# The low parts of 56 weight blocks in the state space part: on VectorE in place of GpSimd

## The chip, the cores and the metric

One core of one Trainium2 chip. The metric is device time in microseconds (us) of one launch, and where several launches were made, their median. Engines are named as in the profile: PE is TensorE's matmul stream and PEld its weight loads, DVE is VectorE, ACT is ScalarE, POOL is GpSimd, SP is SyncE, which issues most DMAs. [...]

## What is computed

One layer of a hybrid diffusion backbone: 512 latent tokens and 256 context tokens of 1024 channels, one combined input projection, a bidirectional gated linear attention branch (GLA, 4 heads) and a bidirectional Mamba-2 branch (SSD, 4 groups of 8 heads), a gated merge, an output projection and a SwiGLU feed-forward part. The change lies in the SSD branch. Cut to it, the reference is:

```python
def _ssd_scan(x, bm, cm, a, s0):
    def step(S, inp):
        xi, bi, ci, ai = inp
        cum = jnp.cumsum(ai, axis=1)
        seg = cum[:, :, None] - cum[:, None, :]
        Lm = jnp.exp(jnp.where(mask, seg, -jnp.inf))
        cb = jnp.einsum('btgn,bsgn->btsg', ci, bi)
        y = jnp.einsum('btsg,btsge,bsgep->btgep', cb, Lm, xi)
        y = y + jnp.einsum('btgn,bgenp->btgep', ci, S) * jnp.exp(cum)[..., None]
        S_new = jnp.exp(cum[:, -1])[..., None, None] * S + jnp.einsum(
            'bsgn,bsge,bsgep->bgenp', bi, jnp.exp(cum[:, -1:] - cum), xi)
        return S_new, y
...
def _mixer(parts, lp, init, conv_fn):
    ...
    o_b, st_bf, st_bb = _bidir(_ssd_scan, (x_f, sb, sc, a_f), (x_b, sb, sc, a_b), init[2], init[3])
    o_b = o_b + lp['d_skip'].reshape(SSM_GROUPS, SSM_HPG, 1) * xh
    o_b = o_b.reshape(Bn, L, SSM_INNER) * jax.nn.silu(z)
    o_b = rms_norm(o_b.reshape(Bn, L, SSM_GROUPS, SSM_INNER // SSM_GROUPS), ...)
    y_b = o_b @ lp['w_pb']
    merged = jax.nn.sigmoid(gate_a) * y_a + jax.nn.sigmoid(gate_b) * y_b
    return merged @ lp['w_out'], (st_af, st_ab, st_bf, st_bb)
```

## The kernel before, in words

All weights come in blocks of 128 partitions x 1024 fp32 numbers. A matmul with fp32 weights is made as three float32r products: the weight is split into a high part `whi` (ACT, a copy that rounds, line 188) and a low part `wlo = raw - whi` (line 189, in `split_w`), the activations likewise, and PE sums hi x hi, hi x lo and lo x hi. `load_raw` (line 176) lets SP fetch the raw block into one of 3 buffers; `whi` and `wlo` have 2 buffers each. A Python list, `split_pool`, says which engine makes the low part: DVE, or POOL while its element is true.

The stages are, with rough times in the profiled execution: loading and the adaptive modulation, GLA heads 0 to 3 (to 400 us), then the SSD branch group by group. `ssd_proj(g)` makes group g's projections: `bm` (1 block), `cm` (1), `xs` (4 blocks) and the gate `z` (4 blocks). Its PE tiles are `l_bm`, `l_xs` (latent tokens), `c_xs` (context tokens) and `r_z` (tokens as rows, four token chunks, two banks). The `xs`, `bm` and `cm` columns go through a convolution on ACT and DVE (`cv_...`, line 663) and are transposed (`tr_x`). `ssd_chain(g)` does the scan in 4 chunks of 128 tokens. Per chunk it makes four tiles `E` (DMA from `cdr`, DVE line 747; a masked copy, line 749), two products `yi` that DVE scales (line 773) and adds to `y` (774), adds the `y` products (775), multiplies by `z` (776), and normalises: ACT sums squares, DVE makes `rv_y` (168), POOL the power `rr_y` (170), DVE scales `y` by it (783). PE then transposes `y` to `yT` (line 501 is a helper through which all these small PE products go), ACT copies it to the high part (788) and DVE makes the low part (789). `proj_back` (lines 632 to 638) multiplies a group's `yT` by the blocks `pb` and DVE adds the result to `acc_b`. It is written behind the projections of the next group, so that it lies beside that group's chain.

After group 3 come the last blocks of the two merge gates (`ga`, `gb`; line 918 on), a transpose `adaT` of the modulation (929), which goes to DRAM and comes back as `sh` and `sc` rows (942), a row of norm weights `n` (DMA on SP, 950) by which DVE multiplies `sc` (952), and `proj_back` of group 3 with the merge of each column block (`tgm`, 969 to 978). Then come the output projection and the feed-forward part, to the end.

[...] PE has 4 banks for the large products (`mm`) and 4 for the small ones (`sm`).

Of the kernel before, what the change touches and what calls it, by code (L numbers as in the profile page):

```python
# [129 lines left out]
def hybrid_layer_kernel(ctx: ExitStack, tc: tile.TileContext, x, xc, wts, vec, rows, up, msk, lvl, out):  # L130
# [48 lines left out]
    split_pool = [False]  # L179
# [497 lines left out]
    def ssd_proj(g):  # L677
        bc = pj.tile([P, 2, SEQ], F32, tag="p4", name=f"bc_{g}")
        lat, cx = proj_cols(("bm", g), True)
        bT = conv_silu(6 * g + 4, lat, cx, f"b_{g}")  # L680
        nc.gpsimd.tensor_copy(bc[:, 0, :], bT[:, 0:SEQ])
        bt = pj.tile([P, 6, P], F32, tag="p3", name=f"bt_{g}")
        to_rows(bT, bt, f"b_{g}")
        lat, _ = proj_cols(("cm", g), False)
        conv_silu(6 * g + 5, lat, None, f"c_{g}", dst=bc[:, 1, :])
        xt = pj.tile([P, 6, 512], F32, tag="x12", name=f"x_{g}")
        for j in range(4):
            lat, cx = proj_cols(("xs", g, j), True)
            xT = conv_silu(6 * g + j, lat, cx, f"x_{g}_{j}")
            to_rows(xT, xt[:, :, j * P:(j + 1) * P], f"x_{g}_{j}")  # L690
        z = [ch.tile([P, 512], F32, tag="z", name=f"z_{g}_{i}", bufs=4) for i in range(4)]
        for c in range(2):
            banks = proj_rows(lambda kh: ("z", g, c, kh), 4)
            for i in range(4):
                pv = banks[i // 2][:, (i % 2) * 256:(i % 2) * 256 + 256]
                zv = z[i][:, c * 256:(c + 1) * 256]
                nc.scalar.activation(zv, pv, AF.Tanh, scale=0.5)
                nc.vector.scalar_tensor_tensor(zv, zv, 1.0, pv, ALU.add, ALU.mult)  # L698
        return bc, bt, xt, z
# [189 lines left out]
    pr, _ = gla_proj(3)  # L889
    early_gate()  # L890
    gla_chain(3, *pr, oH1, oL1)
    split_pool[0] = True
    sp = ssd_proj(0)
    proj_back(lambda c: ("pa", 1, c), oH1, oL1, acc_a, False)
    nc.gpsimd.dma_start(ydr, acc_a)
# [13 lines left out]
    yy = back_pair("yT_3")  # L909
    ssd_chain(3, *sp, *yy)  # L910

    split_pool[0] = False

    for j in range(n_early[0], 8):
        ya = pj.tile([P, SEQ], F32, tag="cva", name=f"ya_{j}")
# [286 lines left out]
```

## Time and profile before

| | |
|---|---|
| median of 3 launches | 1431.89 us (1430.45 to 1432.89) |
| profiled execution, its own time | 1434.66 us |
| its span, first to last instruction | 1432.9 us |
| mean granted clock | 0.981 |
| PE busy | 1357.3 us (95%) |
| DVE busy | 871.0 us (61%) |
| ACT busy | 502.2 us (35%) |
| POOL busy | 465.4 us (32%) |

The profile comes from one execution, taken by the hardware profiler. Its own time is 1.8 us more than its span, which is what lies around the first and the last instruction, and 2.8 us more than the median of the launches without a profiler. Matmuls overlap in the pipeline, so a matmul's printed duration is longer than the distance to the next; the distances between their starts tell the pace. In the name of a group, "x" and a number is a count of instructions, and behind "<-" stands what ended a wait.

### The profile page before, as it was taken

The numbers are of one execution on the slowest core, as the hardware profiler recorded it, in microseconds if no ns is written. First come the engines' busy times: TensorE is split into PE (matmuls) and PEld (weight loads), VectorE is DVE, ScalarE is ACT, GpSimd is POOL, SyncE is SP. The second block draws the span as 40 slices with busy tenths as digits, with TensorE's granted clock in tenths as the row PEclk, the third lists the DMA queues.
The fourth block names the chain that finished last, engine by engine and source line by source line (L and its number), as shares of the span: only waits on it lengthen the run. The fifth ranks groups of instructions, "written<-read, shape, count | busy, mean of one in ns | idle before, by whom it ended". The sixth has DMA issues, their size and how long they took to land.

```text
span 1432.9 us, 19032 instructions
## 1 busy us (share of the span) xinstructions
PE 1357.3 (95%) x7462; PEld 1152.4 (80%) x7462; DVE 871.0 (61%) x1292; ACT 502.2 (35%) x828; POOL 465.4 (32%) x333
## 2 busy tenths in 40 slices
PE   5999999999999999999899899999789999999997
PEld 3798999899888778877877787877578888888886
DVE  4559676563785787569758866766883343433225
ACT  6464333433444223433322342322243222222222
POOL 1355554245234433543253334113651122100001
PEclk9899999999999999999899999999999999999999
DMA  9363323334231343232322332557423333333331
GB/s 367 124 211 108 95 92 112 102 104 144 70 96 60 125 126 96 74 109 83 96 70 84 98 110 78 173 168 253 147 87 101 120 118 116 120 117 91 101 103 73
DMA packets 58010, 169.19 MB, mean 118 GB/s; under 512 B 6064, under 2 KB 10304, under 8 KB 57792
## 3 DMA queue, kind: packets, MB, share of 16 engines
q1 hardware_dynamic: 55328, 157.96, 34.0%
q0 software_dynamic: 2304, 9.64, 2.1%
q8 instruction: 59, 0.97, 0.3%
q10 hardware_dynamic: 288, 0.36, 0.1%
q14 instruction: 31, 0.25, 0.1%
HBM read 156.23 MB, written 11.72 MB: 117 GB/s over the span
## 4 chain that ended last, share of the span: by engine, by line
PE 66%; DVE 15%; DMA 9%; issue 6%; ACT 2%; POOL 2%; SPq 1%; POOLq 0%; DVEq 0%; ACTq 0%
DMA E<-cdr 5%; PE up L1056 3%; PE gate L1055 3%; PE gate L1056 3%; PE up L1055 3%; PE gate L1054 3%; PE up L1054 3%; PE db L204 3%; PE db L206 3%; PE db L205 3%; DVE E L747 2%; PE lv L501 2%; PE r_z L386 1%; PE pb_pb L632 1%; PE pb_pb L634 1%
## 5 line engine op out<-in xcount | busy, mean ns | idle before, releaser
L341 POOL TENSOR_TENSOR raw_ada<-raw_ada,cs 128x1024 f32<-128x1024 f32 x32 | 63.7, 1990 | 279.5 <-DMA raw_ada<-in_wts_dram 227.9
L747 DVE TENSOR_TENSOR E<-E,ebias 128x512 f32<-128x512 f32 x64 | 54.7, 859 | 49.4 <-DMA E<-cdr 49.3
L386 PE MATMUL r_z<-whi_z,hH 128*128 128x256 f32 x256 | 75.7, 298 | 6.6 <-DVE z L698 6.6
L343 POOL TENSOR_TENSOR raw_ada<-raw_ada 128x512 f32<-128x512 f32 x64 | 80.0, 1250 | 4.3
L388 PE MATMUL r_z<-whi_z,hL 128*128 128x256 f32 x256 | 76.9, 301 | 0.0
L387 PE MATMUL r_z<-wlo_z,hH 128*128 128x256 f32 x256 | 74.7, 293 | 0.0
L1054 PE MATMUL gate<-h2H,whi_gate 128*128 128x512 f32 (+1 forms) x192 | 71.8, 374 | 0.0
L1055 PE MATMUL gate<-h2L,whi_gate 128*128 128x512 f32 (+1 forms) x192 | 71.7, 373 | 0.0
L1056 PE MATMUL gate<-h2H,wlo_gate 128*128 128x512 f32 (+1 forms) x192 | 71.5, 373 | 0.0
L189 POOL TENSOR_TENSOR wlo_xs<-raw_xs,whi_xs 128x1024 fp32r<-128x1024 f32 x16 | 43.1, 2693 | 63.8 <-ACT whi_xs L188 63.8
L1056 PE MATMUL up<-h2H,wlo_up 128*128 128x512 f32 x160 | 63.0, 394 | 0.0
L1055 PE MATMUL up<-h2L,whi_up 128*128 128x512 f32 x160 | 62.3, 389 | 0.0
L1054 PE MATMUL up<-h2H,whi_up 128*128 128x512 f32 x160 | 62.2, 389 | 0.0
L189 DVE TENSOR_TENSOR wlo_gate<-raw_gate,whi_gate 128x1024 fp32r<-128x1024 f32 x20 | 33.2, 1661 | 45.2 <-ACT whi_gate L188 45.2
L189 DVE TENSOR_TENSOR wlo_down<-raw_down,whi_down 128x1024 fp32r<-128x1024 f32 x18 | 22.0, 1225 | 62.4 <-ACT whi_down L188 62.3
L386 PEld LDWEIGHTS r_z<-whi_z,hH 128*128 128x128 f32 x256 | 50.9, 200 | 9.2 <-DVE z L698 7.3
L170 POOL TENSOR_TENSOR rr_f<-rv_f,negh 128x1 f32<-128x1 f32 x4 | 2.6, 662 | 168.5 <-DVE rv_f L168 168.5
L189 POOL TENSOR_TENSOR wlo_z<-raw_z,whi_z 128x1024 fp32r<-128x1024 f32 x16 | 39.4, 2462 | 53.5 <-ACT whi_z L188 51.4
L386 PE MATMUL r_v<-whi_v,hH 128*128 128x256 f32 x192 | 55.7, 290 | 1.0 <-ACT whi_v L188 1.0
L205 PE MATMUL db<-wlo_down,fH 128*128 128x512 f32 x142 | 55.2, 389 | 0.0
L206 PE MATMUL db<-whi_down,fL 128*128 128x512 f32 x142 | 55.2, 389 | 0.0
L388 PE MATMUL r_v<-whi_v,hL 128*128 128x256 f32 x192 | 55.1, 287 | 0.0
(475 smaller groups left out, 4460.1 us busy)
## 6 DMA issues: line engine op xcount, KB each, us to landing
raw_ada<-in_wts_dram SPq DMA_DIRECT2D x32, 512.0 KB, 3.6
E<-cdr SPq DMA_DIRECT2D x64, 256.0 KB, 3.4
raw_gate<-in_wts_dram SPq DMA_DIRECT2D x22, 512.0 KB, 3.6
raw_up<-in_wts_dram SPq DMA_DIRECT2D x22, 512.0 KB, 3.5
raw_down<-in_wts_dram SPq DMA_DIRECT2D x22, 512.0 KB, 3.5
aw<-in_wts_dram SPq DMA_DIRECT2D x8, 1024.0 KB, 15.4
raw_xs<-in_wts_dram SPq DMA_DIRECT2D x16, 512.0 KB, 3.6
raw_z<-in_wts_dram SPq DMA_DIRECT2D x16, 512.0 KB, 3.7
```

What stands on the lines that cost most here:

```text
L189: (nc.gpsimd if split_pool[0] else nc.vector).tensor_tensor(lo, raw, hi.bitcast(F32), ALU.subtract)
L205: nc.tensor.matmul(out_, aH, bL, start=False, stop=False)
L206: nc.tensor.matmul(out_, aL, bH, start=False, stop=stop)
L341: nc.gpsimd.tensor_tensor(raw, raw, cs[:, :, 0:1].to_broadcast([P, KD, P]), ALU.mult)
L343: nc.gpsimd.tensor_tensor(raw[:, 0:n, :], raw[:, 0:n, :], raw[:, n:2 * n, :], ALU.add)
L386: nc.tensor.matmul(o, hH[:, kk, tk], hi[:, k, :], start=st, stop=False, skip_group_check=True)
L387: nc.tensor.matmul(o, hH[:, kk, tk], lo[:, k, :], start=False, stop=False, skip_group_check=True)
L388: nc.tensor.matmul(o, hL[:, kk, tk], hi[:, k, :], start=False, stop=sp, skip_group_check=True)
L747: nc.vector.tensor_tensor(ed, ed, ebias[:, d, n, hh].unsqueeze(2).to_broadcast([P, EH, P]), ALU.add)
L1054: nc.tensor.matmul(pts[kj][:, tk], hi[:, k, :], h2H[:, k, tk], start=(k == 0), stop=False)
L1055: nc.tensor.matmul(pts[kj][:, tk], hi[:, k, :], h2L[:, k, tk], start=False, stop=False)
L1056: nc.tensor.matmul(pts[kj][:, tk], lo[:, k, :], h2H[:, k, tk], start=False, stop=(k == KD - 1))
```

## The change

Two lines are taken out, so `split_pool` stays false from the first group's projections to the end of the last group's chain:

```diff
@@ -889,7 +889,6 @@
     pr, _ = gla_proj(3)
     early_gate()
     gla_chain(3, *pr, oH1, oL1)
-    split_pool[0] = True
     sp = ssd_proj(0)
     proj_back(lambda c: ("pa", 1, c), oH1, oL1, acc_a, False)
     nc.gpsimd.dma_start(ydr, acc_a)
@@ -909,7 +908,6 @@
     yy = back_pair("yT_3")
     ssd_chain(3, *sp, *yy)
 
-    split_pool[0] = False
 
     for j in range(n_early[0], 8):
         ya = pj.tile([P, SEQ], F32, tag="cva", name=f"ya_{j}")
```

With that, line 189 runs on DVE for 56 blocks: 40 of the four groups' `bm`, `cm`, `xs` and `z`, 4 of `pa`, 12 of `pb` of groups 0 to 2. The gates `ga` and `gb`, `pb` of group 3 and the output projection had their low parts on DVE already; 4 blocks of the feed-forward part keep theirs on POOL. In the order of the instructions, DVE's rows of line 189 go from 119 to 175 and POOL's from 60 to 4. Up to the first group's projections (about 350 us) and in the feed-forward part each engine keeps its order; between these, the scheduler orders all engines anew. Behind the first line taken out, line numbers are 1 less, behind the second 2 less. Three places show what moved.

DVE, between the end of group 2's chain (`y_2`: its chunk with z tile `z_3_6306`) and group 3's projections (`z_3_7431`, fed by `r_z`). Before:

```order
L774 TENSOR_TENSOR y_2_6967<-y_2_6967,yi_2_6976 128x512
L775 TENSOR_TENSOR y_2_6967<-y_2_6967,y_3_6958 128x512
L747 TENSOR_TENSOR E_0_1_1_7858<-E_0_1_1_7858,ebias 128x512
L776 TENSOR_TENSOR y_2_6967<-y_2_6967,z_3_6306 128x512
L749 COPY_PREDICATED E_0_1_1_7858<-le_78,E_0_1_0_7855 128x512
L747 TENSOR_TENSOR E_1_0_0_7917<-E_1_0_0_7917,ebias 128x512
L168 TENSOR_SCALAR rv_y_6983<-yss_3_6981 128x1
L783 SCALAR_TENSOR_TENSOR y_2_6967<-y_2_6967,rr_y_6985,snw_6680 128x512
```

and of the change:

```order
L774 TENSOR_TENSOR y_2_6967<-y_2_6967,yi_2_6976 128x512
L749 COPY_PREDICATED E_0_1_1_7858<-le_78,E_0_1_0_7855 128x512
L775 TENSOR_TENSOR y_2_6967<-y_2_6967,y_3_6958 128x512
L747 TENSOR_TENSOR E_1_0_0_7917<-E_1_0_0_7917,ebias 128x512
L776 TENSOR_TENSOR y_2_6967<-y_2_6967,z_3_6306 128x512
L189 TENSOR_TENSOR wlo_pb_0_7669<-raw_pb_0_7670,whi_pb_0_7668 128x1024
L747 TENSOR_TENSOR E_1_0_1_7920<-E_1_0_1_7920,ebias 128x512
L168 TENSOR_SCALAR rv_y_6983<-yss_3_6981 128x1
L698 SCALAR_TENSOR_TENSOR z_3_7431<-z_3_7431,r_z_0_0_1_7433 128x256
L749 COPY_PREDICATED E_1_0_1_7920<-le_78,E_1_0_0_7917 128x512
L783 SCALAR_TENSOR_TENSOR y_2_6967<-y_2_6967,rr_y_6985,snw_6680 128x512
```

Between the last sum with `yi` and the scaling of line 783 stand nine rows in place of six, and one of the added ones is a low part. On PE, between the second `yi` product of this chunk and its `yT`, 48 `r_z` matmuls stand where 69 stood.

PE, at the end of the last `gb` block (`l_gb`), where group 3's `pb` (`pb_pb`) begins. Before; here `yT_3_8113`, the transpose of the scan's last chunk, stands 28 matmuls further up, and 52 matmuls lie between the last `yi` and it:

```order
L366 MATMUL l_gb_8507<-hH,wlo_gb_8502 128x512
L929 MATMUL adaT<-idt,ada 96x128
L632 MATMUL pb_pb_0_0_8580<-yT_7804,whi_pb_0_8574 128x512
L633 MATMUL pb_pb_0_0_8580<-yT_7804,whi_pb_0_8574 128x512
L632 MATMUL pb_pb_0_1_8605<-yT_7804,whi_pb_0_8574 128x512
L633 MATMUL pb_pb_0_1_8605<-yT_7804,whi_pb_0_8574 128x512
```

and of the change:

```order
L366 MATMUL l_gb_8507<-hH,wlo_gb_8502 128x512
L501 MATMUL yT_3_8113<-idt,y_3_8092 128x128 x4
L927 MATMUL adaT<-idt,ada 96x128
L632 MATMUL pb_pb_0_0_8580<-yT_7804,whi_pb_0_8574 128x512
L632 MATMUL pb_pb_0_1_8605<-yT_7804,whi_pb_0_8574 128x512
L632 MATMUL pb_pb_1_0_8636<-yT_7804,whi_pb_1_8630 128x512
```

The transpose has moved behind the last `gb` matmul; between the last `yi` product and it are 14 matmuls now, nine of `l_gb` and five small ones of `y`, and `pb` follows it at once.

DVE, in group 3's `proj_back`. Before:

```order
L638 TENSOR_TENSOR acc_b<-acc_b,pb_pb_1_0_8636 128x512
L638 TENSOR_TENSOR acc_b<-acc_b,pb_pb_1_1_8658 128x512
L189 TENSOR_TENSOR wlo_pb_3_8731<-raw_pb_3_8732,whi_pb_3_8730 128x1024
L638 TENSOR_TENSOR acc_b<-acc_b,pb_pb_2_0_8686 128x512
L638 TENSOR_TENSOR acc_b<-acc_b,pb_pb_2_1_8708 128x512
L952 SCALAR_TENSOR_TENSOR sc_0_8546<-sc_0_8546,n_0_8550 128x512
```

and of the change:

```order
L638 TENSOR_TENSOR acc_b<-acc_b,pb_pb_1_0_8636 128x512
L950 SCALAR_TENSOR_TENSOR sc_0_8546<-sc_0_8546,n_0_8550 128x512
L950 SCALAR_TENSOR_TENSOR sc_1_8548<-sc_1_8548,n_1_8553 128x512
L638 TENSOR_TENSOR acc_b<-acc_b,pb_pb_1_1_8658 128x512
L972 SCALAR_TENSOR_TENSOR tgm_0_8619<-tgm_0_8619,yam_8623 128x512
L189 TENSOR_TENSOR wlo_pb_3_8731<-raw_pb_3_8732,whi_pb_3_8730 128x1024
L638 TENSOR_TENSOR acc_b<-acc_b,pb_pb_2_0_8686 128x512
```

The two products `sc`, which wait for the DMA of `n`, have moved ahead of the sum of block `1_1` and of the low part of `pb_3`. On PE, 74 matmuls of `pb` now stand ahead of the first that needs the bank of block `1_1`, and two more ahead of the first that needs the low part of `pb_3`. On SP, a load of `raw_out` that stood between `sc` and `n` now stands behind `n`.

## Rows read from the trace of the kernel before

**Rows 1.** Busy time by stretch, us: PE, PEld, DVE, ACT, POOL (instructions), PEclk, DMA, GB/s

```profile
400.00:850.00 450.00, 422.26 (x2418) 355.51 (x2417) 328.34 (x500) 155.62 (x275) 173.28 (x100) 0.97 0.30 94
850.00:996.00 146.00, 146.00 (x698) 117.64 (x697) 92.09 (x134) 43.01 (x67) 36.25 (x30) 1.00 0.51 166
```

**Rows 2.** PE's waits, 400 to 850 us: in total, times, longest

```profile
PE r_z L386 <- DVE z L698: 6.6, 3, 2.9
PE yT L501 <- DVE y L783: 6.4, 5, 3.0
...
PE tr_x L674 <- ACT bt L675: 1.4, 2, 0.8
...
PE l_xs L361 <- ACT whi_z L188: 1.1, 1, 1.1
PE l_bm L366 <- POOL wlo_bm L189: 1.0, 1, 1.0
...
PE l_bm L361 <- ACT whi_bm L188: 0.6, 1, 0.6
```

**Rows 3.** Line 189 on POOL, 350 to 885 us: length, POOL busy (instructions), PEclk, DMA

```profile
350.00:885.00 535.00, 140.83 (x56) 0.98 0.30 93
```

**Rows 4.** Line 189 on DVE: ns min/median/max, first and last start, form

```profile
L189 DVE TENSOR_TENSOR wlo_up<-raw_up,whi_up x20: 1215/1226/1227, 1083.8 to 1295.2; 128x1024 fp32r<-128x1024 f32 x20
```

**Rows 5.** Three chain operations on DVE: ns min/median/max, first and last start, form

```profile
L747 DVE TENSOR_TENSOR E<-E,ebias x64: 670/692/2294, 407.7 to 940.1; 128x512 f32<-128x512 f32 x64
...
L783 DVE SCALAR_TENSOR_TENSOR y<-y,rr_y,snw x16: 729/752/2876, 492.2 to 961.2; 128x512 f32<-128x512 f32 x16
L773 DVE TENSOR_TENSOR yi<-yi,ecum x32: 676/684/693, 476.9 to 955.0; 128x512 f32<-128x512 f32 x32
```

**Rows 6.** Two of them, grouped: busy us, mean ns | idle before, its releaser

```profile
L747 DVE TENSOR_TENSOR E<-E,ebias 128x512 f32<-128x512 f32 x64 | 54.7, 859 | 49.4 <-DMA E<-cdr 49.3
...
L783 DVE SCALAR_TENSOR_TENSOR y<-y,rr_y,snw 128x512 f32<-128x512 f32 x16 | 20.0, 1250 | 5.0 <-POOL rr_y L170 4.9
```

**Rows 7.** Timeline of DVE and POOL near 678 us: start, us, operation

```profile
678.20 2.34 POOL L189 TENSOR_TENSOR wlo_z<-raw_z,whi_z 128x1024 fp32r<-128x1024 f32 x1
678.27 2.81 DVE L783 SCALAR_TENSOR_TENSOR y<-y,rr_y,snw 128x512 f32<-128x512 f32 x1 [0.40 <-POOL rr_y L170]
```

**Rows 8.** Timeline of DVE at 706 us, in group 2's projections

```profile
705.80 0.69 DVE L747 TENSOR_TENSOR E<-E,ebias 128x512 f32<-128x512 f32 x1 [2.58 <-DMA E<-cdr]
```

**Rows 9.** Busy time by stretch, where the clock is low; columns as in rows 1

```profile
706.00:713.00 7.00, 5.52 (x26) 5.52 (x27) 6.15 (x12) 4.31 (x9) 2.38 (x1) 0.52 0.03 11
```

**Rows 10.** Timeline of PE: two neighbouring matmuls of r_z, then two of l_gb

```profile
716.14 0.28 PE L388 MATMUL r_z<-whi_z,hL 128*128 128x256 f32 x1
716.26 0.28 PE L386 MATMUL r_z<-whi_z,hH 128*128 128x256 f32 x1
...
940.25 0.39 PE L361 MATMUL l_gb<-hH,whi_gb 128*128 128x512 f32 x1
940.48 0.39 PE L362 MATMUL l_gb<-hL,whi_gb 128*128 128x512 f32 x1
```

**Rows 11.** Timeline of the scan's last chunk

```profile
953.51 1.08 PE L501 MATMUL yi<-S_b,bc 128*128 128x512 f32 x2
959.75 0.68 DVE L920 SCALAR_TENSOR_TENSOR tg<-tg,ya 128x512 f32<-128x512 f32 x1
961.17 0.75 DVE L783 SCALAR_TENSOR_TENSOR y<-y,rr_y,snw 128x512 f32<-128x512 f32 x1 [0.67 <-POOL rr_y L170]
966.89 0.60 ACT L788 ACTIVATE yT<-yT 128x512 fp32r<-128x512 f32 x1 [3.65 <-PE yT L501]
```

**Rows 12.** Timeline from adaT to the product sc

```profile
973.06 0.27 PE L929 MATMUL adaT<-idt,ada 128*96 128x128 f32 x1
...
985.34 0.86 SPq L176 DMA_DIRECT2D raw_out<-in_wts_dram  x1
993.02 2.40 DVE L952 SCALAR_TENSOR_TENSOR sc<-sc,n 128x512 f32<-128x512 f32 x1 [2.61 <-DMA n<-in_rows_dram]
```

## The prediction, on record before the changed kernel ran

> **What bounds the kernel now.** I read the page's busy times first, then busy time by stretch, PE's waits, the chain's operations on DVE, and timelines. PE is busy for 95% of the span, so time can be won or lost only where PE waits or runs at the lower clock. The stretch table shows where that is in the part that the change reorders [rows 1]: from 400 to 850 us PE is busy for 422.26 of 450 us, so it waits 27.7 us, and its mean granted clock is 0.97; from 850 to 996 us it waits for nothing, at clock 1.00. Work that the lost 0.03 of clock would have held is 0.03 x 450 = 13.5 us. A perfect 400 to 850 us would thus be 41.2 us shorter, and that is the most that any relief there can give.
>
> PE's waits say what ends the 27.7 us [rows 2]. 6.6 us are `r_z` banks that DVE has not emptied, 6.4 us are `yT`, which waits for DVE's last scaling of `y`; 1.4 + 1.1 + 0.6 = 3.1 us are ended by ACT. The remaining 27.7 - 6.6 - 6.4 - 3.1 = 11.6 us are short waits, most of them for a convolution or chain operation on DVE. Only 1.0 us of them is a wait for a low part from POOL. So the 56 low parts on POOL are hardly ever late; if they cost something, it is through DVE.
>
> That they do, three rows show. An `E` or `y` operation takes 0.69 to 0.75 us in the median but up to 2.9 us [rows 5], while line 773, one of whose two inputs is in PSUM, never passes 0.693 us. One pair shows the long kind [rows 7]: POOL begins a low part of 2.34 us at 678.20, and DVE's line 783, begun 0.07 us later, takes 2.81 us.
>
> [...]
>
> **The change part by part.**
>
> *Added to DVE.* 56 low parts at 1.226 us, the median of the same form on DVE [rows 4], are 56 x 1.226 = 68.7 us.
>
> *Taken from POOL.* 140.83 us [rows 3]. POOL is no bound, and PE waited for it 1.0 us only, which is in the 11.6 us. So this alone is worth nothing beyond the next point.
>
> *Given back to DVE.* The surplus of mean over median is what POOL's work costs [rows 5, 6]: line 747, 64 x (859 - 692) ns = 10.7 us; line 783, 16 x (1250 - 752) ns = 8.0 us. These two groups alone make 18.7 us. DVE is busy for 328.34 of 450 us, 73% [rows 1]. Its share of the added work there is 68.7 x 450/535 = 57.8 us [rows 1, 3]. With nothing given back its load is 86%, with these 18.7 us given back 82%. Neither end is a full engine, and work that DVE does beside PE costs nothing as such; what it costs is decided where PE waits for one DVE instruction.
>
> *PE's short waits.* 11.6 us, between 0 relieved and all. I take all of it: a stall of 2 us in front of a convolution is what makes these waits, and the stretch from 850 us on, where the gates' low parts were already DVE's, has none [rows 1]. Their share of clock I take as 0: the waits are scattered. **-11.6 us.** Bounds for the whole of PE's waiting and clock: 0 and -41.2 us.
>
> *`r_z`.* DVE reaches the evacuation late because an `E` ahead of it waits for its DMA, 2.58 us in one place [rows 8]. The change touches neither that DMA nor its place ahead: **0**; the end is the whole 6.6 us.
>
> *`yT` between groups.* Line 783 becomes 2.81 - 0.75 = 2.1 us shorter where POOL held it [rows 5, 7]. But on the changed order three more rows stand ahead of it between groups 2 and 3: a low part (1.23 us), an `E` operation (0.69) and an evacuation of half width (put at 0.6), some 2.5 us; and PE has 48 `r_z` matmuls to cover it instead of 69, at 0.12 us from one to the next [rows 10]: 21 x 0.12 = 2.5 us less cover. Won 2.1 and lost up to 5.0 for that transition; the other two between groups have a smaller change of cover and win the same. I take **0**: the 6.4 us stay. Ends: -6.4, and +3 for each of three transitions.
>
> *The last chunk.* Before, 52 matmuls covered the way from the last `yi` product to `yT`; now nine `l_gb` and five small ones do. The way takes from 953.51 to 961.17 + 0.75 = 961.92, 8.4 us [rows 11]. The nine matmuls cover 9 x 0.23 = 2.0 us [rows 10], the five small ones about 0.4 (estimate: five at a little under the 0.12 us of an `r_z`), and a `tg` of 0.68 us that stood in the way now stands ahead of it. `pb` needs ACT's copy too, 0.60 us [rows 11], which was covered before. 8.4 - 2.0 - 0.4 - 0.7 + 0.6 = **+5.9 us**. Ends: 0, if DVE ran much ahead, and 8.4.
>
> *`sc`.* Before, DVE started it 993.02 - 973.06 = 20.0 us after `adaT` [rows 12], behind the sums of six blocks, and nothing of PE hung on it. Now it is ahead of the sum of block `1_1`, whose bank PE needs 74 matmuls after `adaT`: 74 x 0.23 = 17.0 us [rows 10], and 0.6 of copy, 17.6. Without the `raw_out` issue of 0.86 us ahead [rows 12] `n` lands at 19.1; two `sc` and the sum, each 0.7 us like line 747 [rows 5], give the bank at 21.2, a wait of 3.6. After 2 more matmuls (0.5 us) PE needs the low part of `pb_3`, behind a `tgm` of 0.7 and itself 1.23: 23.1 against 21.7, a wait of 1.4. **+5.0 us.** Ends: 0, if `n` lands by 15 us, and 7 if it lands later.
>
> *Clock.* Behind a stop of PE the clock falls for a while: in 706 to 713 us PE waited 7 - 5.52 = 1.5 us and had a clock of 0.52 [rows 9], which costs (1 - 0.52) x 7 = 3.4 us. I add one such dip for the stop at the last chunk, where PE stands longest, and half of one, 1.7, for `sc`, whose wait is in two pieces: **+5.1 us**. Ends 0 and 6.8.
>
> **Sum:** -11.6 + 5.9 + 5.0 + 5.1 = +4.4 us on the profiled execution's 1434.66 us. That execution is 2.8 us above the median of the launches, 1431.89 us, so on their scale it is 1436.3; I say **1436 us**, 0.3% slower. This case's own range is 1431 to 1442: the smaller dips on one side, a transition or two on the other.
>
> **The rivals.**
>
> *A, the relief goes further (faster).* With POOL's low parts gone, DVE is early everywhere, and the `yT` waits go with the short ones. Then PE's waits lose 11.6 + 6.4 = 18.0 us and their part of the clock, 13.5 x 18.0/27.7 = 8.8: -26.8. Against it stand 5.9 + 5.0 + 5.1 = 16.0. Net -10.8: 1421 us; with `n` landing early too, 1415. For it: 850 to 996 us, where DVE had just these low parts of the gates and PE waited for nothing [rows 1]. Against it: the shorter cover at the group transitions. It decides once the relief in 400 to 850 us passes 16.0 us.
>
> [...]
>
> *B, DVE becomes the bound (slower).* The stalls do not come back, because POOL's other work, which stays (state products, copies), also holds DVE, and now holds 56 low parts as well, since these read two SBUF inputs like the long rows [rows 5, 7]. At a load of 86% the short waits stay, so that the 16.0 us are not paid for: 1432 + 16 = 1448 us; if the low parts run late too, more. For it: 86% is a mean, and a group's transitions lie above it. Against it: of POOL's 173.28 us in 400 to 850 us some 140.83 x 450/535 = 118 were these low parts [rows 1, 3].
>
> [...] Here DVE is at 73%, so no row shows it saturated before.
>
> *C, `n` lands before `sc` (no difference).* The load of `raw_out` that slowed it has moved behind it. Then 5.0 + 1.7 us go: -11.6 + 5.9 + 3.4 = -2.3, 1430 us. For it: `sc` began 7.7 us after that load's issue, so `n` came slowly beside it [rows 12]. Against it: the `sc` DMAs ahead of `n` still wait for the way through DRAM.
>
> That the change does nothing is out: 56 rows of line 189 change engine in the order.
>
> **How the numbers follow.** Forecast 0.36, A 0.27, B 0.20, C 0.17. A measurement of this kernel tells some 0.2%, 2.9 us, from no change. Faster by more than that (below 1429): 0.25 of A and 0.07 of C, 0.32. Within it (1429 to 1434.8): 0.08 of C, 0.13 of the forecast, 0.02 of A, 0.23. Slower: 0.23 of the forecast, 0.20 of B, 0.02 of C, 0.45. The range takes A with its lower end and B up to a few us over its price: 1415 to 1452 us. Cases of both signs hold most of the chance, so 1431 to 1442 stands beside it.
>
> **What would show it.** DVE's line 189: 56 rows more near 1.23 us. Means of lines 747 and 783 near 0.69 and 0.75 us, and no line of short waits for convolutions between 400 and 850 us: the relief. A PE wait of about 5 us for line 783 ahead of `adaT`, then waits of 3 to 4 us in `pb_3` ended by DVE's line 638 or 189, with low clock behind them: the price. I am wrong if PE stays busy past 960 us, if the `yT` waits at the transitions go (A) or grow (B), or if the mean of line 747 stays near 0.86 us (B).

## The result, and the profile after

The changed kernel took 1415.48 us in the median of 4 runs (1412.36 to 1416.38), the kernel before 1431.17 us beside it: a ratio of 0.9899, 95% interval 0.9877 to 0.9921, 1.1% faster. The forecast of 1436 us was wrong in sign; the time lies at the lower end of the range of 1415 to 1452 us, where rival A with `n` landing early had put it. The profiled execution took 1415.85 us, 18.8 us less than before. Its busy times (us, share of the span, instructions) are:

```profile
PE 1353.3 (96%) x7462; PEld 1151.4 (81%) x7462; DVE 871.4 (62%) x1348; ACT 504.2 (36%) x828; POOL 331.7 (23%) x277
```

DVE has 56 instructions more, most of them near 1.22 us, and is busy for 871.4 us in place of 871.0. What was added has come back in full from operations that no longer take long. The two groups of [rows 6], and line 773 beside them, in the changed kernel (busy us, mean ns | idle before):

```profile
L747 DVE TENSOR_TENSOR E<-E,ebias 128x512 f32<-128x512 f32 x64 | 46.1, 724 | 41.3 <-DMA E<-cdr 41.0
...
L773 DVE TENSOR_TENSOR yi<-yi,ecum 128x512 f32<-128x512 f32 x32 | 21.9, 686 | 19.9 <-PE yi L501 19.8
...
L783 DVE SCALAR_TENSOR_TENSOR y<-y,rr_y,snw 128x512 f32<-128x512 f32 x16 | 12.1, 758 | 1.6 <-POOL rr_y L170 1.4
```

The stretches of [rows 1], and PE's waits between 400 and 850 us, as in [rows 2]:

```profile
400.00:850.00 450.00, 435.56 (x2540) 371.59 (x2539) 342.52 (x558) 162.42 (x284) 58.99 (x53) 0.98 0.31 99
850.00:996.00 146.00, 138.41 (x606) 107.53 (x606) 99.62 (x138) 40.05 (x62) 41.53 (x33) 0.98 0.52 167
```

```profile
PE r_z L386 <- DVE z L698: 6.8, 3, 3.3
PE yT L501 <- DVE y L783: 3.5, 1, 3.5
PE pb_pb L633 <- DVE yT L789: 1.5, 1, 1.5
PE pb_pb L632 <- ACT z L697: 1.0, 1, 1.0
PE oT L501 <- DVE on L612: 1.0, 1, 1.0
PE r_z L386 <- DVE cv_x L663: 0.6, 1, 0.6
```

PE's waits fall from 27.7 to 14.4 us. The waits for convolutions (`cv_`) are gone but for one of 0.6 us, and of the five `yT` waits one is left. `r_z` is as before. From 850 us on, PE waits where it did not: the end of the scan's last chunk, in the timeline (start, us, operation):

```profile
954.27 0.40 PE L366 MATMUL l_gb<-hH,wlo_gb 128*128 128x512 f32 x1
...
957.54 0.75 DVE L783 SCALAR_TENSOR_TENSOR y<-y,rr_y,snw 128x512 f32<-128x512 f32 x1 [0.69 <-POOL rr_y L170]
...
958.43 1.09 PE L501 MATMUL yT<-idt,y 128*128 128x128 f32 x4 [3.76 <-DVE y L783]
959.31 0.42 PE L927 MATMUL adaT<-idt,ada 128*96 128x128 f32 x1
...
960.21 2.07 PE L632 MATMUL pb_pb<-yT,whi_pb 128*128 128x512 f32 x4 [0.47 <-ACT yT L788]
...
968.62 1.65 SPq L948 DMA_DIRECT2D n<-in_rows_dram  x2
...
974.31 1.28 DVE L950 SCALAR_TENSOR_TENSOR sc<-sc,n 128x512 f32<-128x512 f32 x2
```

PE stands for 3.76 + 0.47 us before `pb`, as forecast in kind, but `sc` waits for nothing: `n` is issued 9.3 us after `adaT` (13.2 before), and `sc` runs 15.0 us after it.

Three stretches, each from the first start of one PE tile to the first start of the next, in us, show where the 18.8 us are; the runs of the next section stand beside them (before = kernel before, after = changed kernel). The tile `ob` is the output projection's, so the third stretch begins with the output stage; `db` is the tile of the last products of the feed-forward part (FFN).

| profiled kernel | first `l_bm` to `adaT` | `adaT` to first `ob` | first `ob` to first `db` |
|---|---|---|---|
| before | 615.0 | 21.9 | 310.0 |
| after | 602.1 | 24.8 | 302.1 |
| e1, after + reading shadow | 625.5 | 24.9 | 304.4 |
| e5, after + writing shadow | 597.5 | 24.6 | 304.4 |
| e2, before, fills for low parts | 581.2 | 22.4 | 308.2 |
| e3, group 3 on DVE | 604.2 | 23.4 | 307.2 |
| e4, groups 0 to 2 on DVE | 606.7 | 24.7 | 305.1 |
| e6, before, 4 FFN low parts moved | 614.2 | 21.9 | 309.6 |
| e7, after, 4 FFN low parts moved | 598.5 | 25.3 | 307.1 |
| e8, e7 + row products on DVE | 603.1 | 24.2 | 304.0 |
| e9, before, `tgm` on ACT's queue | 615.6 | 21.9 | 309.6 |
| e10, after, row products on DVE | 596.0 | 24.3 | 303.8 |
| e12, before, row products on DVE | 613.5 | 21.9 | 301.2 |
| e13, before + gate pair | 601.6 | 37.8 | 307.0 |
| e14, after + gate pair | 578.3 | 31.9 | 306.0 |
| e11, e14 + row products on DVE | 577.6 | 32.0 | 299.2 |

From before to after: -12.9, +2.9 and -7.9 us; with 0.8 us ahead of the first `l_bm` and nothing behind the first `db`, that is the change of the span. Each row is one execution. In the order of the kernel before (before, e6, e9, e12) the first stretch takes 613.5 to 615.6 us, in that of the changed kernel with nothing reading beside it (after, e5, e7, e8, e10) 596.0 to 603.1: the 12.9 us are one figure out of a spread of 7 us.

### The profile page after: what moved, and what is told of

It is laid out like the page before. It is cut to its first block, busy times and chain, and to the rows that moved or that the text cites. A ratio compares the mean times of both kernels' runs of the same rounds, so it can differ in the third digit from the quotient of the medians.

```text
span 1414.1 us, 19042 instructions
## 1 busy us (share of the span) xinstructions
PE 1353.3 (96%) x7462; PEld 1151.4 (81%) x7462; DVE 871.4 (62%) x1348; ACT 504.2 (36%) x828; POOL 331.7 (23%) x277
## 4 chain that ended last, share of the span: by engine, by line
PE 80%; DVE 9%; DMA 6%; ACT 2%; issue 2%; POOL 1%; SPq 0%; POOLq 0%; DVEq 0%; ACTq 0%
DMA E<-cdr 3%; PE up L1054 3%; PE gate L1053 3%; PE up L1053 3%; PE gate L1054 3%; PE gate L1052 3%; PE up L1052 3%; PE db L204 3%; PE db L206 3%; PE db L205 3%; PE yi L501 2%; PE l_xs L361 2%; PE l_xs L366 2%; PE l_xs L362 2%; PE pb_pb L632 2%; PE pb_pb L633 2%
## 5 line engine op out<-in xcount | busy, mean ns | idle before, releaser
L747 DVE TENSOR_TENSOR E<-E,ebias 128x512 f32<-128x512 f32 x64 | 46.1, 724 | 41.3 <-DMA E<-cdr 41.0
L632 PE MATMUL pb_pb<-yT,whi_pb 128*128 128x512 f32 x128 | 53.3, 421 | 1.5 <-ACT z L697 1.0
L387 PE MATMUL r_v<-wlo_v,hH 128*128 128x256 f32 x192 | 54.6, 284 | 0.0
L633 PE MATMUL pb_pb<-yT,whi_pb 128*128 128x512 f32 x128 | 52.8, 413 | 1.5 <-DVE yT L789 1.5
```

Source lines behind the costliest of these rows:

```text
L387: nc.tensor.matmul(o, hH[:, kk, tk], lo[:, k, :], start=False, stop=False, skip_group_check=True)
L632: nc.tensor.matmul(pt, hi[:, k, cl], aH[:, k, :], start=(k == 0), stop=False)
L633: nc.tensor.matmul(pt, hi[:, k, cl], aL[:, k, :], start=False, stop=False)
```

## The experiments

Medians are in us; ratios are to the kernel before, timed on the same chip, with their 95% intervals.

**e1 and e5: POOL's reads, or POOL's queue, or the new order?** To the changed kernel, a "shadow" on POOL is added behind each of the 56 low parts (the lines that switch it on and off are left out here). In e1 it reads SBUF:

```diff
+            if shadow[0]:
+                hf = hi.bitcast(F32).rearrange("p k c -> p (k c)")[:, 0:896]
+                nc.gpsimd.tensor_tensor(dmy_, hf, hf, ALU.subtract)
```

> The changed kernel, with one extra POOL subtraction (896 columns, two SBUF inputs, result unused) behind each of the 56 low parts that DVE now makes; every engine keeps the changed kernel's order but for a few rows. Theory L (the time came from POOL's reads no longer holding up DVE): lines 747 and 783 go back to means above 0.80 and 1.0 us, and 8 to 20 us of the 15.7 us won come back, mostly between 358 us and adaT: 1423 to 1436 us. Theory O (it came from the new order of instructions and DMAs): the means may rise, but the time stays within 3 us of 1415.5 us.

In e5 the last line is replaced:

```diff
-                nc.gpsimd.tensor_tensor(dmy_, hf, hf, ALU.subtract)
+                nc.gpsimd.tensor_copy(dmy_[:, 0:1], hf[:, 0:1])
+                nc.gpsimd.memset(dmy_, 0.0)
+                nc.gpsimd.memset(dmy_, 0.0)
+                nc.gpsimd.memset(dmy_, 0.0)
```

> The changed kernel, with POOL work behind each of the 56 low parts that reads almost nothing: a copy of one column of the high part, then three fills of 896 columns. The order of all engines is the changed kernel's but for a few rows, as with the subtraction that read SBUF (1439.7 us). Theory L (POOL's reads hold DVE up): no cost, 1412 to 1420 us, means of lines 747 and 783 as in the changed kernel. Theory Q (POOL's own queue is what costs: state products, y and rr_y wait behind the low parts): the cost comes back, 1430 to 1440 us.

e1 took 1439.68, a ratio of 1.0067 [1.0041, 1.0092], and e5 1415.30, 0.9881 [0.9846, 0.9915]. The added lines shift the numbers: lines 747 and 783 are 752 and 788 in e1, 755 and 791 in e5. The groups of operations of e1 (busy us, mean ns | idle before):

```profile
L752 DVE TENSOR_TENSOR E<-E,ebias 128x512 f32<-128x512 f32 x64 | 55.0, 864 | 38.3 <-DMA E<-cdr 38.2
...
L788 DVE SCALAR_TENSOR_TENSOR y<-y,rr_y,snw 128x512 f32<-128x512 f32 x16 | 14.2, 890 | 1.6 <-POOL rr_y L170 1.4
```

one group of its shadow (ns min/median/max, first and last start):

```profile
L194 POOL TENSOR_TENSOR dmy<-whi_xs x16: 1680/2255/3031, 373.4 to 787.6; 128x896 bf16<-128x896 f32 x16
```

and the same two views of e5:

```profile
L755 DVE TENSOR_TENSOR E<-E,ebias 128x512 f32<-128x512 f32 x64 | 44.6, 701 | 42.5 <-DMA E<-cdr 42.3
...
L791 DVE SCALAR_TENSOR_TENSOR y<-y,rr_y,snw 128x512 f32<-128x512 f32 x16 | 12.2, 760 | 2.2 <-POOL rr_y L170 2.0
```

```profile
L196 POOL MEMSET dmy<- x56: 844/845/847, 354.1 to 849.1; 128x896 bf16 x56
```

With its reading shadow POOL is busy for 461.6 us, 129.9 more than in the changed kernel, with the writing one for 521.7, 190.0 more. The longer one costs nothing: DVE is busy for 870.1 us in e5, 871.4 without a shadow. The one that reads costs 24 us, DVE is busy for 912.4 us with the same 1348 instructions, and line 747 has its 864 ns back. This is more than the 8 to 20 us that were expected, while line 783, at 890 ns, stayed below the 1.0 us expected.

The single operations show it as well. Of line 747's 64, those that began while a low part or a shadow of POOL ran took 1.57 us in the mean in the kernel before (12 of them) and 1.58 in e1 (11); the 17 that began while e5's shadow ran took 0.69 us, none over 0.695. Line 773, with one input in PSUM, stayed at 0.693 us or less in all three.

So POOL's queue falls as a cause, and the reads stand. The new order alone isn't enough for the gain, since e1 has it and is slow; what the order adds by itself no run measures.

PE's waits in e1, 400 to 880 us, show what a DVE does that has the 56 low parts and is held up too:

```profile
PE yT L506 <- DVE y L788: 12.4, 4, 7.0
PE r_z L391 <- DVE z L703: 10.1, 3, 4.0
```

**e2: the reads taken from the kernel before.** The lines that set `split_ms` for the 56 blocks are left out here.

```diff
-            (nc.gpsimd if split_pool[0] else nc.vector).tensor_tensor(lo, raw, hi.bitcast(F32), ALU.subtract)
+            if split_ms[0]:
+                nc.gpsimd.memset(lo.bitcast(F32), 0.0)
+            else:
+                (nc.gpsimd if split_pool[0] else nc.vector).tensor_tensor(lo, raw, hi.bitcast(F32), ALU.subtract)
```

> The kernel before, but POOL fills each of the 56 low parts with zeros, which reads nothing from SBUF; the low parts of these weights are left out of the result. The order of PE and DVE differs from both kernels. Theory L: the means of lines 747 and 783 fall to about 0.70 and 0.78 us without any low part moving to DVE, and the time is that of the changed kernel or less, 1402 to 1418 us. Theory O: less than half of the gain, 1424 to 1433 us.

e2 took 1397.11, a ratio of 0.9766 [0.9738, 0.9794], faster than forecast. Its busy times:

```profile
PE 1343.1 (96%) x7462; PEld 1144.2 (82%) x7462; DVE 812.1 (58%) x1292; ACT 502.4 (36%) x828; POOL 380.0 (27%) x333
```

DVE runs the same 1292 instructions as before in 812.1 us in place of 871.0: 58.9 us were time in which it was held. The order differs here too, so it isn't shown that the 33 us of gain are the reads' alone.

**e3 and e4: by groups.** In the kernel before (e3):

```diff
+    split_pool[0] = False
     sp = ssd_proj(3)
```

and in the changed kernel (e4):

```diff
+    split_pool[0] = True
     sp = ssd_proj(3)
...
     ssd_chain(3, *sp, *yy)
+    split_pool[0] = False
```

> Only from group 3's projections on (10 blocks of group 3 and the 4 blocks of pb of group 2) are the low parts made by DVE, the rest by POOL. If the stage of the output projection (64.2 us from the first ob to the first gate matmul before, 54.5 after) gained from the order that group 3 sets, it gains here as well, some 8 to 10 us, while the stretch from 358 us to adaT keeps 610 to 616 us (615.1 before, 602.3 after): 1418 to 1426 us. If that stage gained for another reason: 1427 to 1433 us.

> The complement: low parts of groups 0 to 2, pa and pb of groups 0 and 1 on DVE, those of group 3 and of pb of group 2 on POOL. Theory L: the stretch from the first bm to group 3's first bm (397.2 us before, 374.2 after) stays at 372 to 380 us, the last chunk's wait of 3.8 us ahead of adaT goes, the output stage is as before (62 to 65 us): 1411 to 1420 us. Theory O: the order of the end is redone, so no forecast below 1420 us.

e3 took 1420.82, 0.9919 [0.9891, 0.9947], within its forecast, and e4 1421.84, 0.9934 [0.9910, 0.9959], 1.8 us above that of theory L. The places are not those forecast. In e3 the way from the first `ob` to the first gate matmul gained 2.8 us and not 8 to 10, and the way to `adaT` 10.8 us. In e4 the way to group 3's first `l_bm` kept 375.5 us (397.2 before, 374.2 after), as theory L has it, but the wait for the last `yT` stayed, 3.2 us, and the output stage gained where it was to stay: 56.0 us to the first gate matmul. The gains of the two parts, 8.9 and 7.8 us, make 16.7, about the whole 15.7. So no group holds the gain alone.

**e6, e7: the 4 low parts left on POOL, e9: SP's queue.** In the kernel before (e6) and the changed one (e7):

```diff
-    split_pool[0] = True
     for j in range(2):
         ahead[("gate", j)] = load_w(("gate", j))
```

and in the kernel before (e9):

```diff
-        nc.sync.dma_start(ta, tdr[:, j, 0])
-        nc.sync.dma_start(tb, tdr[:, j, 1])
+        nc.scalar.dma_start(ta, tdr[:, j, 0])
+        nc.scalar.dma_start(tb, tdr[:, j, 1])
```

> The kernel before, with only the 4 low parts of the feed-forward part moved from POOL to DVE; the order up to the output projection stays. If the stage from the first ob to the first gate matmul (64.2 us before, 54.5 after) loses time because these 4 collide with hn on DVE: PE's wait of 5.3 us for hn goes and the time falls by 4 to 7 us, 1423 to 1427 us. If hn is late for another reason (merges that come late): less than 2 us.

> The changed kernel with the same 4 low parts on DVE as well. If they cost through collisions with hn, a little more is left here too (waits of 0.8 and 1.5 us near the first gate matmul): 1411 to 1415 us. Otherwise within 2 us of 1415.5 us.

> The kernel before, with the loads of the merge gates (tgm, two per column block) issued by ACT's DMA queue in place of SP's; the order of DVE and POOL is the same, that of PE but for two rows. Theory S (in the output projection the merges come late because on SP two loads of raw_out that wait 8 us for a buffer stand ahead of the tgm loads, and the changed kernel's order mended that): the way from the first ob to the first db matmul, 310.0 us before and 302.1 after, falls to 302 to 306 us and the time by 3 to 8 us, 1424 to 1429 us. Theory D (it is DVE's order and its stretched operations): within 2 us of before.

e6 took 1431.05, 0.9990 [0.9974, 1.0006]; e7 1419.29, 0.9902 [0.9880, 0.9923], the changed kernel's own ratio; e9 1432.76, 1.0007 [0.9990, 1.0024]. The gain that each was to bring did not come: neither the collision with `hn` (the normalised rows ahead of the feed-forward part) nor the loads behind `raw_out` explain the third stretch, which stayed at 309.6 us in e6 and e9. In e6 PE's wait for `hn` did fall, from 5.3 to 2.5 us, and the first gate matmul came 4.3 us earlier after the first `ob`, but at the first `db` 0.4 us were left of that.

**e8, e10, e12: the row products.** Line 187 multiplies each `raw_out` block by a row, on POOL, between the merges:

```diff
-                nc.gpsimd.tensor_tensor(raw[:, 0, :], raw[:, 0, :], row, ALU.mult)
+                nc.vector.tensor_tensor(raw[:, 0, :], raw[:, 0, :], row, ALU.mult)
```

> As the last one, and the 8 row products of raw_out (line 187, 2.4 us each on POOL) made by DVE too. Theory L: DVE's stretched merges (2.2 to 2.9 us in place of 0.7) and low parts of the output projection shorten by more than the 8 x 1.2 us that DVE gets: PE's waits in the output projection, 6.6 us, fall by 2 to 5 us, 1407 to 1413 us. If DVE is too full there: 1413 to 1420 us.

> The changed kernel with the 8 row products of raw_out made by DVE; the 4 low parts of the feed-forward part stay on POOL. With both on DVE 1412.7 us were measured, with the latter alone 1419.3. If the two add up: 1407 to 1411 us. If the row products only mended what the moved low parts did: 1412 to 1416 us.

> The kernel before, with the 8 row products of raw_out (line 187) made by DVE in place of POOL; the order up to the output projection stays. Theory L for the output stage (merges and low parts on DVE are held up there by POOL's reads in these products, and the changed kernel's order only met them less): the way from the first ob to the first db matmul, 310.0 us before, falls to 301 to 305 us, the time to 1423 to 1427 us. If the merges are late for their own order: 308 to 311 us, and no change of the time.

e8 (on e7) took 1412.66, 0.9857 [0.9831, 0.9883], within theory L's forecast. e10 (on the changed kernel) took 1413.79, 0.9872 [0.9847, 0.9897], which can't be told from the change alone: the two moves do not add up to 1407 to 1411 us. e12 (on the kernel before) took 1424.70, 0.9949 [0.9931, 0.9968], and the stretch from the first `ob` to the first `db` falls from 310.0 to 301.2 us, both as theory L had it. In the timeline of the kernel before:

```profile
999.16 6.18 POOL L187 TENSOR_TENSOR raw_out<-raw_out,g1r 128x1024 f32<-128x1024 f32 x2
...
1000.22 2.88 DVE L978 SCALAR_TENSOR_TENSOR mt<-tgm,mt 128x512 fp32r<-128x512 f32 x1
...
1003.02 2.88 DVE L975 SCALAR_TENSOR_TENSOR tgm<-tgm,acc_b 128x512 f32<-128x512 f32 x1
```

and the same operations in e12:

```profile
998.26 1.21 DVE L187 TENSOR_TENSOR raw_out<-raw_out,g1r 128x1024 f32<-128x1024 f32 x1
999.40 0.68 DVE L978 SCALAR_TENSOR_TENSOR mt<-tgm,mt 128x512 fp32r<-128x512 f32 x1
1000.00 0.68 DVE L975 SCALAR_TENSOR_TENSOR tgm<-tgm,acc_b 128x512 f32<-128x512 f32 x1
```

With the order up to the output projection unchanged, moving 8 reading products off POOL wins as much there as the whole change did. So that stage lost its time to these products. DVE's merges beside them are held (2.88 us against 0.68), but the product itself is shorter on DVE as well (1.2 us against 2.7 on POOL), and no run separates the two. That the changed kernel wins there although its row products stay on POOL goes with its order (e1 and e5, in the same order, have 304.4 us, with and without a reading shadow); which rows of the order make it so was not isolated.

**e11, e13, e14: work behind the last chain.** One pair `ga`, `gb` comes behind the last chain:

```diff
     pr, _ = gla_proj(3)
-    early_gate()
     gla_chain(3, *pr, oH1, oL1)
```

> The kernel before, with one pair of merge-gate blocks made behind the last chain instead of in the GLA part, POOL still making the 56 low parts. If those 18 us of the run with the pair moved came from the pair's new place alone, they come here too: 1412 to 1420 us. If they need DVE free of POOL's reads, so that the work behind the chains can be used: within 6 us of 1431 us.

> The changed kernel with the same pair moved and the row products on POOL. With the row products on DVE it took 1395.3 us, and these were worth about 2 us without the pair: 1395 to 1401 us. If the two only work together: above 1405 us.

> As the last one, and one pair of merge-gate blocks (ga, gb of one column block) is made behind the last chain instead of in the GLA part, so that 48 more large matmuls lie at the end. If the 4 us that PE waits for the last yT (and the low clock behind it) come from too little work behind the last chain: 4 to 8 us less than the last one, 1399 to 1407 us. If the scheduler spends the blocks ahead of the last yi instead: no change, or a loss of a few us in the GLA part.

e13 (kernel before) took 1433.52, 1.0011 [0.9995, 1.0027]. e14 (changed kernel) took 1404.28, 0.9818 [0.9788, 0.9849]. e11 (e14 with row products on DVE) took 1395.30, 0.9743 [0.9718, 0.9769], **the fastest version that leaves nothing out, 2.6% under the kernel before**. e14 missed its forecast of 1395 to 1401, and e11 won more than forecast. PE's waits between 400 and 960 us, in e11:

```profile
PE tr_x L674 <- DVE ct_x L667: 4.4, 3, 2.4
PE pb_pb L634 <- DVE wlo_pb L189: 3.1, 1, 3.1
...
PE yT L501 <- DVE y L783: 0.8, 1, 0.8
```

and in e13:

```profile
PE yT L501 <- DVE y L783: 16.0, 8, 3.5
PE tr_x L674 <- DVE ct_x L667: 5.6, 3, 2.5
```

The pair's place pays with the change and not without it: in e13 `yT` waits eight times, in e14 and e11 once. More went than the last `yT` wait: the `r_z` waits of 6.8 us that DVE's line 698 ended went too, and why the new order is rid of those was not tried.

## Why the prediction was wrong

The sum was +4.4 us; the two profiled executions differ by -18.8. By the stretches of the table it had -2.3 us up to `adaT` (-11.6 + 5.9, and the dip of 3.4), +6.7 up to the first `ob`, and nothing behind it. Measured were -12.9, +2.9 and -7.9 us. So three terms failed: the relief up to `adaT`, which depends on how much DVE gets back, the price of `sc`, and the output stage, which was put at nothing.

*Added to DVE, 68.7 us: right.* The moved low parts have medians of 1.218 to 1.226 us. Some were held themselves, the longest to 3.42 us.

*Given back to DVE, 18.7 us, load 82 to 86%: the step that failed.* It counted two groups of operations. These came out as priced, 8.6 + 7.9 = 16.5 us, but others were held as well, line 717 most of all (before, then after):

```profile
L717 DVE TENSOR_TENSOR xc_b<-x,coef 128x512 f32<-128x512 f32 x16 | 23.6, 1480 | 14.0 <-ACT x L675 14.0
...
L717 DVE TENSOR_TENSOR xc_b<-x,coef 128x512 f32<-128x512 f32 x16 | 11.9, 757 | 7.7 <-ACT x L675 7.7
```

Lines 749 and 774 gave back 7.9 and 6.4 us more. In all, 68.7 - 0.4 = 68.3 us came back (e2 shows 58.9 us by another way), so that the load from 400 to 850 us went from 73 to 342.52/450 = 76%. By the prediction's own measure, the surplus over the median, taken over every form in place of two, 49 us were held between 400 and 850 us, and 8 are left. The sum had no term for them beyond the waits that PE's list showed.

*Short waits, -11.6 us: right in kind.* All but 0.6 us of the waits for convolutions went, and the waits besides the two that follow fell from 14.7 to 4.1 us. *`r_z`, 0: right*, 6.6 and 6.8 us. *`yT` between groups, 0: wrong.* 6.4 became 3.5 us; the cover did shrink as the order shows, but DVE, held less, reached line 783 in time at all but one place. The granted clock from 400 to 850 us, as a share of full speed, went from 0.97 to 0.98.

*The last chunk, +5.9 us, and its dip, +3.4: right in kind.* PE stood for 3.76 + 0.47 = 4.2 us, and from 957 to 964 us the granted clock was 0.55 in the mean (columns as in [rows 1]):

```profile
957.00:964.00 7.00, 5.09 (x14) 3.92 (x15) 1.73 (x3) 0.60 (x1) 1.08 (x2) 0.55 0.94 348
```

It was 0.50 from 957.63 to 964.46 us, where `pb_pb` matmuls began 0.43 us apart, and 1.00 behind that, where they began 0.23 us apart. 5.15 us of the 0.50 lie behind `adaT`; half of them, about 2.6 us, is their cost (estimate), which with the 0.47 us is about the +2.9 us up to the first `ob`.

*`sc`, +5.0 and +1.7 us: wrong.* PE did not wait for it: `n` had landed 15.0 us after `adaT` at the latest, the end that was priced at 0. The prediction took `n`'s old way less one issue of 0.9 us, but `n` was issued 3.9 us earlier, since the `sh` and `sc` loads ahead of it also kept SP for 2.8 us in place of 5.5. Rival C had `n` early; whether the moved `raw_out` load is the reason no run shows.

*The output stage, 0: left out without a reason.* It gave 7.9 us. The prediction looked at PE's waits between 400 and 996 us only, though the order of all engines is new up to the feed-forward part. DVE was held there too: its low parts `wlo_out` fell from 1.97 to 1.30 us in the mean and `hn` (line 1018, then 1016) from 1.40 to 0.93.

Up to `adaT`, 10.6 us more came than the sum had. PE's waits there fell by 8.1 us in place of 11.6 - 5.9 = 5.7, which makes 2.4. The time at a granted clock of 0.50 fell from 23.9 to 22.2 us, half of which is -0.9 us (estimate) in place of +3.4, and makes some 4; it is chance in part, since executions in the changed kernel's order had between 9.4 and 22.2 us of it. The last 4 us are in PE's busy time, 582.4 us in place of 587.3 for the same 3257 matmuls. Which delays these were is not shown; a sum over listed waits can't hold them.

Rival A had the mechanism, and e1 and e5 show it; its 1415 us are right partly by luck, since its relief did not contain the output stage. Rival B, that other reads of POOL keep DVE held, is refuted by line 747's mean of 724 ns, 32 above its median before.

## What to carry to other kernels

Where two engines hold each other up, as POOL and DVE did here, work moved from the one to the other is not simply added to the second's load (of 68.7 us added to DVE, 68.3 came back): first subtract everything in which the second was held, over all its forms, and over every stage that the new order reaches. A shadow of the moved work, once reading and once only writing, in an order that stays the same, tells the hold from the queue in two runs. When such a hold is gone, earlier compromises of order (here, gate blocks made early) are worth trying again: the same move that gave nothing before gave 11 us after.

## What was not expected of the hardware

In e1 POOL's operations are held as well as they hold. A shadow and DVE's low part of the same block wait for the same `whi`, and in both of these pairs the one that starts second is the long one. Where the shadow starts 0.09 us ahead, DVE's operation takes 2.70 us and the shadow 1.70; where DVE starts 0.11 us ahead, POOL's takes 2.65 and DVE's 1.23:

```profile
588.71 1.70 POOL L194 TENSOR_TENSOR dmy<-whi_pb 128x896 bf16<-128x896 f32 x1 [2.12 <-ACT whi_pb L190]
588.80 2.70 DVE L191 TENSOR_TENSOR wlo_pb<-raw_pb,whi_pb 128x1024 fp32r<-128x1024 f32 x1
...
688.36 1.23 DVE L191 TENSOR_TENSOR wlo_z<-raw_z,whi_z 128x1024 fp32r<-128x1024 f32 x1 [0.50 <-ACT whi_z L190]
688.47 2.65 POOL L194 TENSOR_TENSOR dmy<-whi_z 128x896 bf16<-128x896 f32 x1 [1.40 <-ACT whi_z L190]
```

The 56 shadow subtractions of e1 took between 1.67 and 3.03 us, while the 168 fills of the same 896 columns in e5 took 0.84 to 0.86. And in e5 the fills cost DVE's two-input operations nothing measurable: line 747 had a mean of 701 ns with 168 fills in the kernel, less than the 724 ns without.
